# Keys' factor as a logarithm inside the exponent, decays summed per 128 tokens, and bias-fed exponentials for the two coarsest levels, in a gated linear recurrence

## The chip, the cores and the metric

The kernel runs on one core of a Trainium2 chip. The metric is the device time of one execution in microseconds. TensorE (PE) multiplies matrices into PSUM, VectorE (DVE), ScalarE (ACT) and GpSimd (POOL) work on tiles of 128 partitions, and SyncE (SP) issues most of the loads. Every engine takes its own instructions strictly in order.

## The reference

Three transformer blocks run one after the other on 512 tokens of 1024 features. The change touches one branch of the first: a gated linear recurrence with 4 heads of 128 key and 128 value columns, once forward and once backward over the tokens.

```python
def gla_chunkwise(q, k, v, log_f):
    """S_t = diag(f_t) S_{t-1} + k_t v_t^T ; o_t = S_t^T q_t, chunkwise."""
...
        def hgrn_direction(f_logit, lb, reverse):
            f = lb + (1.0 - lb) * jax.nn.sigmoid(f_logit.astype(f32))
            log_f = heads(jnp.log(f), HG_KDIM)
            kh = heads(1.0 - f, HG_KDIM)
            ...
        o_hg = hgrn_direction(f_fw, lb_all[0, layer], False) + hgrn_direction(f_bw, lb_all[1, layer], True)
```

So the weight of token s in the output of token t is a sum over the key columns of q_t times (1 - f_s) times the exponential of a difference of cumulated logarithms of f. All else in the three blocks (latent attention, a mixture of 64 experts, retention, sparse attention, a second recurrence, feed-forwards) is untouched.

## The kernel before

The kernel never walks through the tokens. For each head it builds the whole 512x512 matrix of weights, `At`, by levels. A level L cuts the tokens into pairs of neighbouring blocks of L tokens. Between the two blocks of a pair the decay goes through the pair's middle, so it splits into a factor of the query token and a factor of the key token; the two halves then carry one matmul. Levels 256 and 128 fill the parts of `At` off the diagonal blocks (lines 531 and 537); levels 1, 2, 4, ... 64 fill the four 128x128 blocks on the diagonal (line 551), and `copy_predicated` with a mask (line 556) picks from each level's product the entries that belong to it. A product without any decay, of the queries `q2` and the sum of both directions' keys `ksum` (line 546), gives the diagonal itself.

`hgrn_prepare` does one head's preparation: three column products of the input projection (line 150), the queries `q2`, `sg[d]` = 1 - f for the two directions d (tiles `hs`), the logarithm of f (tiles `hf`, ACT `Ln`, line 482), and its cumulated sum `gs[d]` over all 512 tokens (tiles `hg`, a DVE scan with a zero in front, line 486).

`hgrn_level` makes the factors of one level. Four POOL subtractions of 128x256 (lines 509 and 510) put "middle minus own" or "own minus middle" into `heq` and `hek`, two ACT exponentials of 128x512 follow (lines 511 and 512), and three DVE products: `hq` = queries times `heq` (128x512, line 513) and, for each direction, its half of `hk` = keys times `hek` (128x256, line 515). The four tiles have three buffers each. That is done nine times for each of four heads.

`hgrn_head` runs the levels of a head and their matmuls, moves the sums from PSUM to `At` (ACT, lines 532, 539, 553, 559), and multiplies `At` by the values (line 563). `o_emit` normalizes the head's output with a chain of small DVE instructions and a POOL product (line 634), and PE transposes it (line 639) a little later.

The order around it: `weave` alternates the steps of `hgrn_head` with steps of other PE work, `FILL` (1.4, 1.4, 1.5, 0.5) steps for each step of heads 0 to 3. The other work is the next head's `hgrn_prepare` and then a piece of other products: `mem` products of the second block in heads 0 and 1 (lines 1363 to 1365 and 187 to 189), the `ple` projection in head 2 (lines 187 to 189, evicted by ACT at line 2751), a gate in head 3. Every weight is loaded as `raw` and split into a rounded part `wh` (ACT, line 68) and a rest `wl` (DVE, line 69). A scheduler then sets the final order of each engine's queue from the order in which the code issues; the queues themselves run in order.

Behind the recurrence come the latent attention with the other gates, the merge, the router, and the experts, whose weights `w` are loaded by SP (lines 987 and 996).

## Time and profile before

| | |
|---|---|
| time, median of 3 runs (range) | 3288.96 us (3280.67 to 3289.59) |
| time of the profiled execution | 3286.79 us |
| its span, first to last instruction | 3284.7 us |
| PE, DVE, ACT, POOL busy | 93%, 55%, 31%, 10% of the span |
| the recurrence's four heads | 106.9 to 300.8 us of the span |

PE is busy nearly everywhere, so a microsecond counts only where PE stands still or runs at a lower granted clock. The four heads are one of the few stretches where it does; there POOL, of 10% over the whole span, is nearly always busy. A head is read here from the start of its first level's matmuls, or of the product with the values that closes the head before it, to its own product with the values.

### The profile page before, as it was taken

The page shows a single profiled execution, that of the slowest core. Times are in us where ns is not written, and L with a number is a line of the kernel's source. Part 1 is how long each engine was busy: PE and PEld are TensorE (multiplying, and loading weights), DVE is VectorE, ACT ScalarE, POOL GpSimd, SP SyncE. Part 2 cuts the span into 40 slices and gives each one's busy share as a digit, 9 for nine tenths or more (in the row PEclk, how much of TensorE's full clock was granted, in tenths as well). Part 3 has the DMA queues.
Part 4 walks back from the last instruction along what each step waited for, and adds up shares of the span by engine and source line. Part 5 has one row for each costly group of instructions (what it writes and reads, how often), then busy time and mean ns, then how long its engine had stood idle before and what let it go on. Part 6 is the DMA issues. An engine that isn't in the chain of part 4 may idle for free.

```text
span 3284.7 us, 40559 instructions
## 1 busy us (share of the span) xinstructions
PE 3061.4 (93%) x16321; PEld 2332.6 (71%) x16321; DVE 1790.4 (55%) x3211; ACT 1019.1 (31%) x1550; POOL 337.1 (10%) x395
## 2 busy tenths in 40 slices
PE   9888999788777899999999999999999889999999
PEld 7687777434333688888767778888876767688887
DVE  3777765733432634345974656543477775464443
ACT  3556543110000422223413432322223244232221
POOL 0654101000000000001100320000023210000000
PEclk9889999899888999999999999999999989799999
DMA  4222224699899432333322244323333410123222
GB/s 144 82 71 83 65 65 194 274 421 421 367 421 417 145 102 91 102 105 114 103 90 84 90 154 160 103 91 102 103 95 105 136 51 17 50 90 103 95 91 84
DMA packets 240985, 466.38 MB, mean 142 GB/s; under 512 B 24722, under 2 KB 163380, under 8 KB 216732
## 3 DMA queue, kind: packets, MB, share of 16 engines
q1 hardware_dynamic: 230956, 431.95, 36.5%
q0 software_dynamic: 9840, 31.82, 2.8%
q8 instruction: 130, 2.13, 0.3%
q14 instruction: 59, 0.48, 0.0%
HBM read 441.17 MB, written 22.56 MB: 141 GB/s over the span
## 4 chain that ended last, share of the span: by engine, by line
PE 43%; DVE 6%; issue 1%; ACT 1%; POOL 0%; DMA 0%; DVEq 0%; ACTq 0%; POOLq 0%
PE pg L150 20%; PE pg L188 4%; PE pg L189 4%; PE pg L187 4%; PE pg L2094 1%; DVE wl L69 1%; DVE nprod L2353 1%; PE pt L2084 1%; PE pg L176 1%; PE pg L175 1%; PE pg L174 1%; PE pa L2070 1%; PE pg L2488 1%; PE pg L2487 1%; PE pt L1419 0%
## 5 line engine op out<-in xcount | busy, mean ns | idle before, releaser
L69 DVE TENSOR_TENSOR wl<-raw,wh 128x2048 fp32r<-128x2048 f32 (+3 forms) x211 | 440.2, 2087 | 458.3 <-ACT wh L68 458.2
L68 ACT ACTIVATE wh<-raw 128x2048 fp32r<-128x2048 f32 (+3 forms) x214 | 368.8, 1724 | 703.1 <-PE pg L150 352.0
L150 PE MATMUL pg<-x2h,wh 128*128 128x512 f32 (+2 forms) x1136 | 441.8, 389 | 0.0
L150 PE MATMUL pg<-x2h,wl 128*128 128x512 f32 (+2 forms) x1136 | 440.2, 388 | 0.0
L150 PE MATMUL pg<-x2l,wh 128*128 128x512 f32 (+2 forms) x1136 | 439.2, 387 | 0.0
L150 PEld LDWEIGHTS pg<-x2h,wl 128*128 128x128 f32 (+1 forms) x1136 | 212.8, 187 | 49.2 <-issue 7.3
L150 PEld LDWEIGHTS pg<-x2l,wh 128*128 128x128 f32 (+1 forms) x1136 | 212.8, 187 | 47.6 <-issue 6.4
L150 PEld LDWEIGHTS pg<-x2h,wh 128*128 128x128 f32 (+1 forms) x1136 | 212.9, 187 | 45.6 <-issue 3.0
L188 PE MATMUL pg<-wl,hh 128*128 128x512 f32 x608 | 238.5, 392 | 0.0
L189 PE MATMUL pg<-wh,hl 128*128 128x512 f32 x608 | 237.6, 391 | 0.0
L187 PE MATMUL pg<-wh,hh 128*128 128x512 f32 x608 | 236.6, 390 | 0.0
L1155 PE MATMUL pa<-w,mscr 128*32 128x512 f32 x1024 | 171.0, 669 | 50.4 <-DMA w<-w 48.1
L1155 PEld LDWEIGHTS pa<-w,mscr 128*32 128x32 f32 x1024 | 42.4, 121 | 154.9 <-issue 140.1
L188 PEld LDWEIGHTS pg<-wl,hh 128*128 128x128 f32 x608 | 114.2, 188 | 25.4 <-DVE wl L69 0.8
L187 PEld LDWEIGHTS pg<-wh,hh 128*128 128x128 f32 x608 | 114.1, 188 | 25.1
L189 PEld LDWEIGHTS pg<-wh,hl 128*128 128x128 f32 x608 | 114.2, 188 | 23.8
L187 PE MATMUL pg<-wh,x2h 128*128 128x512 f32 (+1 forms) x288 | 101.5, 353 | 1.0 <-ACT x2h L232 1.0
L189 PE MATMUL pg<-wh,x2l 128*128 128x512 f32 (+1 forms) x288 | 100.8, 350 | 0.0
L188 PE MATMUL pg<-wl,x2h 128*128 128x512 f32 (+1 forms) x288 | 100.4, 349 | 0.0
L150 PE MATMUL pg<-x1h,wh 128*128 128x512 f32 x224 | 90.9, 406 | 1.1 <-ACT po L2751 0.7
L150 PE MATMUL pg<-x1l,wh 128*128 128x512 f32 x224 | 90.9, 406 | 0.0
L150 PE MATMUL pg<-x1h,wl 128*128 128x512 f32 x224 | 90.2, 405 | 0.0
(882 smaller groups left out, 6006.4 us busy)
## 6 DMA issues: line engine op xcount, KB each, us to landing
w<-w SPq DMA_DIRECT2D x188, 1024.0 KB
raw<-w_in SPq DMA_DIRECT2D x45, 1024.0 KB
raw<-ffn_w_in SPq DMA_DIRECT2D x44, 1024.0 KB
raw<-w_ff SPq DMA_DIRECT2D x16, 1024.0 KB
raw<-w_ff SPq DMA_DIRECT2D x20, 768.0 KB
raw<-w_in SPq DMA_DIRECT2D x24, 512.0 KB
raw<-w_out SPq DMA_DIRECT2D x12, 1024.0 KB
raw<-ffn_w_out SPq DMA_DIRECT2D x16, 768.0 KB
```

Of the source, the lines that this page charges most:

```text
L68: nc.scalar.activation(h, t, AF.Copy)
L69: (nc.gpsimd if i in self.slow else nc.vector).tensor_tensor(l, t, f32v(h), op=OP.subtract)
L150: nc.tensor.matmul(p, w[:, c, s], x[:, c, t], start=first, stop=last)
L174: nc.tensor.matmul(p[:, t], wh[:, c, s], xh[:, c, t], start=c == 0, stop=False)
L175: nc.tensor.matmul(p[:, t], wh[:, c, s], xl[:, c, t], start=False, stop=False)
L176: nc.tensor.matmul(p[:, t], wl[:, c, s], xh[:, c, t], start=False, stop=c == nk - 1)
L187: nc.tensor.matmul(p, xh[:, c, t], wh[:, c, :ncol], start=start and c == 0, stop=False)
L188: nc.tensor.matmul(p, xh[:, c, t], wl[:, c, :ncol], start=False, stop=False)
L189: nc.tensor.matmul(p, xl[:, c, t], wh[:, c, :ncol], start=False, stop=stop and c == nk - 1)
L1155: nc.tensor.matmul(ph[s], xt[:, c, s], w[:, :, c], start=c == 0, stop=c == DC - 1)
L2070: mm(ps[s], qT[:, c + 4 * s, i * P:(i + 1) * P], kT[:, s, j, :W], start=j == 0, stop=j == 1)
L2084: nc.tensor.transpose(pt[:, j], prs[s][:, j * P:(j + 1) * P], k.ident)
```

## The change

In `hgrn_prepare` the logarithm of the keys' factor is taken too: `sg[d]` becomes ln(1 - f + 1e-30) (two more ACT `Ln` of 128x512 a head). The cumulated sums restart every 128 tokens: `g` has the shape 128 x 4 x 129, filled by four DVE scans of 128 columns for each direction in place of one of 512, and a tile `htw` of two columns holds the sums of blocks 0 and 1. POOL adds or subtracts these sums and the keys' logarithms once a head (two operations of 128x512), so that `ys` holds the keys' whole exponent but for the middle. `ksum` moves from `hgrn_head` into `hgrn_prepare`.

In `hgrn_level` the keys' factor then comes straight out of the exponential, and the two products of line 515 go. For levels 1 to 64 POOL keeps two subtractions (keys), DVE takes the other two (queries), and two ACT exponentials of 128x512 and one DVE product follow as before. For levels 128 and 256 nothing is subtracted: the middle is the bias of the exponential, in eight ACT instructions of 128x128 for each of the two levels. Results are written in place, so two tile names with four buffers each replace four with three.

```diff
     for d in range(2):
         S.activation(fs[d], fs[d], AF.Ln)
     for d in range(2):
-        g = t(f"hg{d}", (P, T + 1))
-        nc.gpsimd.memset(g[:, 0:1], 0.0)
-        V.tensor_tensor_scan(g[:, 1:], k.one.to_broadcast([P, T]), fs[d], 0.0, op0=OP.mult, op1=OP.add)
+        S.activation(sg[d], sg[d], AF.Ln, bias=k.tiny)
+    two = t("htw", (P, 2))
+    for d in range(2):
+        g = t(f"hg{d}", (P, NT, P + 1))
+        G.memset(g[:, :, 0:1], 0.0)
+        for b in range(NT):
+            V.tensor_tensor_scan(g[:, b, 1:], k.one.to_broadcast([P, P]), fs[d][:, b * P:(b + 1) * P], 0.0,
+                                 op0=OP.mult, op1=OP.add)
+        V.tensor_tensor(two[:, d:d + 1], g[:, 0, P:], g[:, 1, P:], op=OP.add)
         gs.append(g)
-    out.append((q2, sg, gs))
+    G.tensor_tensor(blk(sg[0]), gs[0][:, :, 1:], blk(sg[0]), op=OP.subtract)
+    G.tensor_tensor(blk(sg[1]), gs[1][:, :, 0:P], blk(sg[1]), op=OP.add)
+    out.append((q2, ksum, gs, sg, two))
...
-    for d in range(2):
...
-        G.tensor_tensor(cut(first)[:, :, 0], mid, own[:, :, 0], op=OP.subtract)
-        G.tensor_tensor(cut(second)[:, :, 1], own[:, :, 1], mid, op=OP.subtract)
-    S.activation(eq, eq, AF.Exp)
-    S.activation(ek, ek, AF.Exp)
-    V.tensor_tensor(q, q2, eq, op=OP.mult)
-    for d in range(2):
-        V.tensor_tensor(cut(kk)[:, :, d], cut(ks[d])[:, :, d], cut(ek)[:, :, d], op=OP.mult)
+    if L >= P:
+        for b0 in range(0, NT, 2 * L // P):
+            n = L // P
+            m = b0 + n
+            for b in range(b0, m):
+                e0, e1 = (g[:, b, P:] if b == m - 1 else two[:, d:d + 1] for d, g in enumerate((g0, g1)))
+                S.activation(kb[:, b], y0[:, b], AF.Exp, scale=-1.0, bias=e0)
+                S.activation(qb[:, b], own1[:, b], AF.Exp, scale=-1.0, bias=e1)
+            S.activation(qb[:, m], own0[:, m], AF.Exp)
+            S.activation(kb[:, m], y1[:, m], AF.Exp)
+            if n == 2:
+                S.activation(qb[:, m + 1], own0[:, m + 1], AF.Exp, bias=g0[:, m, P:])
+                S.activation(kb[:, m + 1], y1[:, m + 1], AF.Exp, bias=g1[:, m, P:])
+    else:
...
+        G.tensor_tensor(cut(kb)[:, :, :, 0], mid0, cut(y0)[:, :, :, 0], op=OP.subtract)
+        G.tensor_tensor(cut(kb)[:, :, :, 1], cut(y1)[:, :, :, 1], mid1, op=OP.subtract)
+        V.tensor_tensor(cut(qb)[:, :, :, 0], mid1, cut(own1)[:, :, :, 0], op=OP.subtract)
+        V.tensor_tensor(cut(qb)[:, :, :, 1], cut(own0)[:, :, :, 1], mid0, op=OP.subtract)
+        S.activation(q, q, AF.Exp)
+        S.activation(kk, kk, AF.Exp)
+    V.tensor_tensor(q, q2, q, op=OP.mult)
```

The scheduler makes new queues of this in the four heads; behind them every queue stands as before. Three places follow.

The first place is POOL and DVE at the start of head 0 (levels 256, 128, 1, 2, ... in this order). `hg`, `hs`, `heq` and `hek` are the tiles named above, `hac` is the tile in which the diagonal blocks are collected. POOL before:

```order
L546 TENSOR_TENSOR hks_828<-hs_40_648,hs_41_649 128x512
L509 TENSOR_TENSOR hek_759<-hg_48_752 128x256
L510 TENSOR_TENSOR heq_758<-hg_48_752 128x256
L509 TENSOR_TENSOR hek_798<-hg_48_752 128x2x128
L510 TENSOR_TENSOR heq_797<-hg_48_752 128x2x128
L509 TENSOR_TENSOR heq_758<-hg_49_755 128x256
L510 TENSOR_TENSOR hek_759<-hg_49_755 128x256
```

POOL in the changed kernel:

```order
L484 TENSOR_TENSOR hks_752<-hs_40_650,hs_41_651 128x512
L498 TENSOR_TENSOR hs_40_650<-hg_50_759,hs_40_650 128x512
L499 TENSOR_TENSOR hs_41_651<-hg_51_766,hs_41_651 128x512
L532 TENSOR_TENSOR hek_876<-hg_50_759,hs_40_650 128x256
L533 TENSOR_TENSOR hek_876<-hs_41_651,hg_51_766 128x256
```

Levels 256 and 128 are gone from POOL's queue; two operations of 128x512 stand ahead of level 1, which is the first that POOL serves. DVE before, at the same place:

```order
L486 SCALAR_TENSOR_TENSOR hg_48_752<-one,hf_46_744 128x512
L486 SCALAR_TENSOR_TENSOR hg_49_755<-one,hf_47_747 128x512
L513 TENSOR_TENSOR hq_760<-hq_39_647,heq_758 128x512
L515 TENSOR_TENSOR hk_761<-hs_40_648,hek_759 128x256
L515 TENSOR_TENSOR hk_761<-hs_41_649,hek_759 128x256
```

DVE in the changed kernel:

```order
L494 SCALAR_TENSOR_TENSOR hg_50_759<-one,hf_46_746 128x128 x4
L496 TENSOR_TENSOR htw_758<-hg_50_759 128x1
L494 SCALAR_TENSOR_TENSOR hg_51_766<-one,hf_47_749 128x128 x4
L496 TENSOR_TENSOR htw_758<-hg_51_766 128x1
L538 TENSOR_TENSOR heq_775<-hq_39_649,heq_775 128x512
L534 TENSOR_TENSOR heq_875<-hg_51_766 128x256
L535 TENSOR_TENSOR heq_875<-hg_50_759 128x256
L534 TENSOR_TENSOR heq_900<-hg_51_766 128x128x2
```

Between the scans and level 256's matmuls DVE now has one product where it had three; the subtractions of levels 1 and 2 stand behind it.

The second place is ACT at the end of head 0, where it moves the collected blocks `hac` to `At` (line 559 before, line 580 now), behind exponentials that already belong to head 1. `mo` is an eviction of a `mem` product. Before:

```order
L2737 ACTIVATE mo_1106<-pg_1081 128x256
L512 ACTIVATE hek_1286<-hek_1286 128x512
L511 ACTIVATE heq_1358<-heq_1358 128x512
L512 ACTIVATE hek_1359<-hek_1359 128x512
L511 ACTIVATE heq_1387<-heq_1387 128x512
L512 ACTIVATE hek_1388<-hek_1388 128x512
L2737 ACTIVATE mo_1159<-pg_1134 128x256
L559 ACTIVATE At<-hac_827 128x4x128
```

In the changed kernel, the last wide exponential of head 0 first:

```order
L537 ACTIVATE hek_1165<-hek_1165 128x512
...
L528 ACTIVATE hek_1245<-hs_58_796,hg_85_999 128x128
L522 ACTIVATE hek_1282<-hs_57_795,hg_84_992 128x128
L2760 ACTIVATE mo_1161<-pg_1136 128x256
L523 ACTIVATE heq_1281<-hg_85_999 128x128
L524 ACTIVATE heq_1281<-hg_84_992 128x128
L525 ACTIVATE hek_1282<-hs_58_796 128x128
L522 ACTIVATE hek_1282<-hs_57_795,hg_84_992 128x128
L68 ACTIVATE wh_1266<-raw_1057 128x1024
L580 ACTIVATE At<-hac_840 128x4x128
```

What stands ahead of the eviction were exponentials that read what POOL had just subtracted; now it is 13 narrow ones, whose inputs are made once for the head, two evictions of `mo` and one weight split.

The third place is PE at the same moment: the product with the values reads `At` (line 563 before, line 584 now). Before:

```order
L1364 MATMUL pg_1181<-mhl,wh_1047 128x256
L1365 MATMUL pg_1181<-mhl,wl_1048 128x256
L531 MATMUL pa_1259<-hq_1248,hk_1249 128x256
L563 MATMUL pg_1210<-hv,At 128x128 x16
L531 MATMUL pa_1259<-hq_1248,hk_1249 128x256
L531 MATMUL pa_1263<-hq_1248,hk_1249 128x256 x2
```

In the changed kernel:

```order
L572 MATMUL pa_1124<-heq_1115,hek_1116 128x128 x4
L572 MATMUL pa_1173<-heq_1164,hek_1165 128x128 x4
L1387 MATMUL pg_1179<-mhl,wh_1053 128x256
L1388 MATMUL pg_1179<-mhl,wl_1054 128x256
L1386 MATMUL pg_1179<-mhl,wh_1053 128x256
L1387 MATMUL pg_1179<-mhl,wh_1053 128x256
L1388 MATMUL pg_1179<-mhl,wl_1054 128x256
L554 MATMUL pa_1255<-heq_1244,hek_1245 128x256 x2
L554 MATMUL pa_1259<-heq_1244,hek_1245 128x256 x2
L584 MATMUL pg_1208<-hv,At 128x128 x16
```

All four of head 1's first matmuls now stand ahead of head 0's product with the values, where one stood; the last two levels of head 0 stand later among the `mem` products than they did.

## Rows read from the trace of the kernel before

**Rows 1.** The page's first line: the span.

```profile
span 3284.7 us, 40559 instructions
```

**Rows 2.** Busy time by stretch, heads 0 to 3: length, busy (count), clock, DMA.

```profile
core 0: us, PE busy (x) PEld busy (x) DVE busy (x) ACT busy (x) POOL busy (x), PEclk, DMA share, GB/s
106.92:160.64 53.72, 37.53 (x224) 33.60 (x224) 47.57 (x56) 30.33 (x49) 45.25 (x57) 0.85 0.18 53
160.64:217.32 56.68, 48.46 (x283) 44.12 (x283) 40.83 (x61) 29.88 (x44) 32.17 (x39) 0.86 0.23 70
217.32:280.06 62.74, 54.30 (x292) 47.38 (x293) 49.93 (x77) 40.15 (x67) 47.31 (x56) 0.93 0.24 71
280.06:300.84 20.78, 19.06 (x118) 16.54 (x117) 14.95 (x38) 9.37 (x28) 5.89 (x5) 1.00 0.40 136
```

**Rows 3.** PE in order of time: start, us, what, [idle before, releaser].

```profile
111.89 3.78 PE L531 MATMUL pa<-hq,hk 128*128 128x256 f32 x8 [4.97 <-DVE hk L515]
...
160.64 6.00 PE L563 MATMUL pg<-hv,At 128*128 128x128 f32 x32 [6.58 <-ACT At L559]
...
176.28 1.11 PE L639 MATMUL pt<-ident,osq 128*128 128x128 f32 x4 [3.09 <-POOL osq L634]
...
269.78 0.50 PE L187 MATMUL pg<-wh,phl 128*128 128x512 f32 x1 [3.10 <-ACT po L2751]
...
280.06 3.74 PE L563 MATMUL pg<-hv,At 128*128 128x128 f32 x32
```

**Rows 4.** DVE, POOL, ACT by line: ns shortest/median/longest, first and last start, form.

```profile
L513 DVE TENSOR_TENSOR hq<-hq,heq x36: 655/844/1121, 110.1 to 295.3; 128x512 f32<-128x512 f32 x36
L515 DVE TENSOR_TENSOR hk<-hs,hek x72: 395/828/1526, 111.0 to 296.9; 128x256 f32<-128x256 f32 x72
L486 DVE TENSOR_TENSOR_SCAN hg<-one,hf x8: 1203/1216/2295, 103.3 to 256.4; 128x512 f32<-128x512 f32 x8
L509 POOL TENSOR_TENSOR hek<-hg x36: 607/792/2661, 105.6 to 284.6; 128x256 f32<-128x256 f32 x36
L546 POOL TENSOR_TENSOR hks<-hs,hs x4: 1282/1680/3320, 103.6 to 254.5; 128x512 f32<-128x512 f32 x4
L511 ACT ACTIVATE heq<-heq x36: 612/630/638, 109.4 to 283.3; 128x512 f32<-128x512 f32 x36
L539 ACT ACTIVATE At<-pa x16: 258/278/301, 118.6 to 274.5; 128x128 f32<-128x128 f32 x16
L482 ACT ACTIVATE hf<-hf x8: 630/632/637, 102.6 to 255.7; 128x512 f32<-128x512 f32 x8
L482 ACT ACT_TABLE_LOAD  x6: 1283/1283/1283, 101.3 to 254.4; - x6
L511 ACT ACT_TABLE_LOAD  x4: 1283/1283/1283, 104.1 to 257.1; - x4
```

**Rows 5.** Start of head 0, DVE and ACT in order of time.

```profile
103.33 3.38 DVE L486 TENSOR_TENSOR_SCAN hg<-one,hf 128x512 f32<-128x512 f32 x2
...
109.42 0.63 ACT L511 ACTIVATE heq<-heq 128x512 f32<-128x512 f32 x1 [4.04 <-POOL heq L509]
...
110.08 0.99 DVE L513 TENSOR_TENSOR hq<-hq,heq 128x512 f32<-128x512 f32 x1 [3.38 <-ACT heq L511]
```

**Rows 6.** End of head 0, DVE and ACT in order of time.

```profile
156.52 0.72 DVE L556 COPY_PREDICATED hac<-lev,pa 128x512 f32<-128x512 int32 x1
...
157.66 0.63 ACT L511 ACTIVATE heq<-heq 128x512 f32<-128x512 f32 x1 [2.55 <-POOL heq L509]
...
159.97 0.62 ACT L559 ACTIVATE At<-hac 128x512 f32<-128x512 f32 x1
```

**Rows 7.** Behind the heads: a wait in SP's queue, and two stretches (columns of rows 2).

```profile
SPq L987 <- PE pg L189: 26.0, 1, 26.0
...
580.00:600.00 20.00, 10.67 (x71) 10.31 (x71) 19.27 (x41) 0.80 (x2) 0.00 (x0) 0.62 0.22 93
900.00:1000.00 100.00, 82.24 (x512) 40.07 (x512) 35.71 (x56) 8.87 (x15) 0.00 (x0) 0.90 1.01 421
```

35 lines of the change are left out of this document (18 added, 17 removed).

## The prediction

> **What bounds the kernel now.** I read first the busy time by stretch, because PE is busy 93% of the span and only a stretch where it stands can give anything back. Over heads 0 to 3 the length less PE's busy time is 16.2, 8.2, 8.4 and 1.7 us, together 34.6 [rows 2]. The granted clock is 0.85, 0.86 and 0.93 there, so part of the busy time ran at 1.2 instead of 2.4 GHz: busy time times the missing share is 37.5 x 0.15 = 5.6, 48.5 x 0.14 = 6.8 and 54.3 x 0.07 = 3.8 us, together 16.2 [rows 2]. Read it off one product: the 32 matmuls with the values take 6.00 us behind a wait of 6.58 us, and 3.74 us where PE came out of steady work [rows 3]. So 34.6 + 16.2 = 50.8 us is all that any change of these heads could give.
>
> Next, who lets PE wait. The order in time names DVE's keys product at the start (4.97 us), ACT's copy into `At` at the end of head 0 (6.58), POOL's product before the transposes (3.09), ACT's eviction `po` (3.10) [rows 3]. Behind these names stands one pair: in head 0 DVE is busy 47.6 and POOL 45.3 of 53.7 us, in head 2 49.9 and 47.3 of 62.7 [rows 2]. The ACT waits lead back to it too: the last masked copy of head 0 ends at 157.24, yet its move to `At` starts at 159.97, because an exponential ahead of it in ACT's queue had waited 2.55 us for POOL [rows 6]. And the two lengthen each other: a 128x256 product on DVE takes 0.395 us at best and 0.828 as a rule, a 128x512 one 0.655 and 0.844, a POOL subtraction 0.607 and 0.792 [rows 4].
>
> **POOL's part.** A head now has 36 subtractions and one sum: 36 x 0.792 + 1.68 = 30.2 us. It keeps 14 subtractions and gets three operations of 128x512 priced as the sum: 14 x 0.792 + 3 x 1.68 = 16.1 [rows 4]. 14 us a head go; they are no term of the sum by themselves, since PE never waits for POOL alone, but they halve what DVE collides with.
>
> **DVE's part.** At unchanged durations a head has 9 x 0.844 + 18 x 0.828 + 2 x 1.216 = 24.9 us of products and scans [rows 4]. Of the 18 half products none stay, and 14 half subtractions come, of the same form and count of inputs, so at the same 0.828. A scan of 128 columns is not in the trace: a quarter of 1.203 is 0.30, and a quarter of the longest, 2.295, is 0.57. Between 256 and 512 columns the products grow by 0.26 us, which leaves 0.135 fixed; that gives (1.203 - 0.135) / 4 + 0.135 = 0.40, near the lower end, and 0.135 for each of two one-column sums. So 9 x 0.844 + 14 x 0.828 + 8 x 0.40 + 0.3 = 22.7: 2.2 us less a head; with 0.57 it is 0.9 less, with 0.30 it is 3.0.
> Then the collisions. The excess over the shortest is 9 x 0.189 + 14 x 0.433 = 7.8 us in the new list. With POOL at 16.1 / 30.2 = 53% of its work I take 53% of it, 4.1: another 3.6 us less. It is nothing if the two still meet as often, and 7.8 if they never meet. DVE's head gets shorter by 5.8 us (0.9 to 10.8).
>
> **Head 0** runs at DVE's pace, so the 5.8 us count whole. Its start: the second scan ended at 106.7, then POOL's subtractions let ACT start at 109.42, and PE started at 111.89 [rows 3, 5]. Now eight scans end at about 107.5 (103.33 + 8 x 0.40 + 0.3, and some collision with the sum on POOL). POOL's sum runs from 103.6 until 105.3; of its two new operations the second has to await the scans and ends at 109.2, at 1.68 [rows 4]. Four logarithms from 102.6 on and the table load, 4 x 0.632 + 1.283 [rows 4], end at 106.4 and hold nothing up. The eight narrow exponentials, 0.278 each, of which the last three wait for the second operation, end at 110.0, the queries' product at 110.7. That is 1.2 us earlier than 111.89; with POOL at its shortest 1.28 us it is 2.5. I take 1.5. Four column matmuls stand ahead of it now, which fill part of the wait and are missing later: nothing. Its end: of the 2.7 us between masked copy and move to `At` I take 1.5, since 13 narrow exponentials (13 x 0.278 = 3.6 us, fed once a head) stand where eight POOL-fed ones stood. And half of the clock's 5.6, 2.8, for waits that get short. Together 5.8 + 1.5 + 1.5 + 2.8 = 11.6.
>
> **Heads 1 and 2** don't run at DVE's pace throughout (40.8 of 56.7 and 49.9 of 62.7 us busy [rows 2]); the normalization's chain of small instructions, ACT's evictions and PE's own work take their share. I take half of PE's standing, 4.1 and 4.2, and a third of the clock, 2.3 and 1.3: 6.4 and 5.5. **Head 3** has 1.7 us in all: nothing.
>
> **ACT's part.** Added are 8 logarithms of 0.632 us, 64 narrow exponentials of 0.278 in place of 16 wide ones of 0.63, and two table loads of 1.283, since the new logarithms stand apart from the exponentials of levels 16 to 64 in two heads: 5.1 + 7.7 + 2.6 = 15.4 us in 194 us in which ACT is busy 110 [rows 2, 4]. Most lies beside PE's filling products. On the path are the loads at the end of heads 0 and 2, where the last levels' exponentials follow them: 2.6 if both end last, 0 if the `mem` and `ple` products cover them. I take 1.5.
> The trace shows a load of 1.283 us ahead of logarithms six times and ahead of exponentials four times [rows 4], so each change between the two costs one here. The Trainium skill (ScalarE: Activation LUTs, section "Table sets: the hidden batching unit") says that one set holds exponential and logarithm together and that the pair needs one load. By that rule the two new loads would be free and the term would be 0; the rows speak otherwise, and the sum goes by them.
>
> **What it meets later.** Nothing behind the heads is reordered. The first load of expert weights waits 26.0 us for a matmul of PE, the DMA is at 0.22 of its share while PE stands for the router, and only then the experts run at 421 GB/s [rows 7]. So a load-bound stage follows, but it starts when PE gets there, and what the heads gain stays gained.
>
> **Sum.** 11.6 + 6.4 + 5.5 - 1.5 = 22.0 us. The profiled execution took 3286.79 us, 2.1 more than its span of 3284.7 [rows 1] and 2.2 less than the median of 3288.96: 3286.8 - 22.0 = 3264.8, so **3265 us**. Taking DVE's ends (0.9 and 10.8 for 5.8 in head 0, and a quarter or three quarters of the standing of heads 1 and 2), the same working gives 3252 to 3276.
>
> **Rivals.** *The pair takes turns (faster still).* The best durations next to the usual ones say that DVE and POOL hardly run side by side at all. If so, their shortest durations add up: before, POOL 36 x 0.607 + 1.28 = 23.1 and DVE 9 x 0.655 + 18 x 0.395 + 2 x 1.203 = 15.4, 38.5 us a head; after, 14 x 0.607 + 3 x 1.28 = 12.3 and 9 x 0.655 + 14 x 0.395 + 8 x 0.40 + 0.3 = 14.9, 27.2 [rows 4]. Three heads shorter by 11.3 each, the start's 1.5 and half of the clock's 16.2 are 43.5: 3243 us. Against it: in head 1 PE is busy 48.5 of 56.7 us and cannot lose 11 without the clock [rows 2]. Chance 0.12.
> The Trainium skill (SBUF — State Buffer, section "Who interferes with whom") states this as a rule: a DVE instruction with two SBUF inputs and a GpSimd instruction that reads SBUF exclude each other for the whole instruction. The rows' 0.395 against 0.828 us agree with waiting, but no row shows that it is for the whole of it. By the same rule DVE's new subtractions stay in the collision, which speaks against a change that only moves work from POOL to DVE.
>
> *It moves the work only (no change).* POOL's 14 us go, but DVE still has 25 instructions a head that meet POOL, and keeps its place as the queue that ends last. Then only the 0.9 us a head of three heads with dear scans and the start's 1.2 remain, less 1.5 on ACT: 2.4 us, 3284. For it: DVE stands for only 6.1 of head 0's 53.7 us, 3.4 of them at the start [rows 2, 5]. Chance 0.20.
>
> *ACT ends last (slower).* At each of three head ends the move to `At` stands behind 13 narrow exponentials, two `mo` and a weight split. If POOL's two new operations for the next head come late (they queue behind the old head's level 64), the whole group runs after them: 3.6 + 0.8 + 1.0 = 5.4 us, and 1.3 for a table load, 6.7 at three ends, 20.1 us; against it the start, 1.5, and DVE's gain in head 0 of 5.8, with clock 2.0: 10.8 slower, 3298. It decides from where the product with the values waits more than some 4 us for ACT at all three ends; in head 0 it does so already. Against it: ACT has 84 idle us in the heads [rows 2]. Chance 0.08.
>
> **How the numbers follow.** The forecast has 0.60. About 0.3%, 10 us, is what a measurement of this kernel can tell from no change. Faster by more: the forecast and the taking of turns, 0.72; within: 0.20; slower: 0.08. The range has to reach into the no-change case and half into the fast one: 3245 to 3285 leaves out 0.08 slow, half of 0.12 fast and a quarter of 0.20.
>
> **What will show it.** Right: PE's standing over the heads falls from 34.6 to about 17 us; POOL is busy half as long; the half subtractions on DVE have a median near 0.6 us; a 128-column scan takes about 0.4; `At` at the end of head 0 makes PE wait under 3 us. Wrong: subtractions on DVE at 0.83 and PE's waits unchanged (no change), waits of PE for ACT's move to `At` of over 4 us at three ends (slower), or a first expert load that doesn't come earlier by what the heads gained.

## The result, and the profile after

The changed kernel takes 3264.51 us (median of 5 runs, 3260.15 to 3269.12), the kernel before 3282.08 us beside it (5 runs): a ratio of 0.994 with a 95% interval of 0.9923 to 0.9958. The forecast was 3265 us, with a range of 3245 to 3285, so the time and the sign came as predicted. That the time came within half a microsecond is luck: the forecast took 22.0 us from a profiled execution of 3286.79 us, while the kernel before has a median of 3282.08 us beside the change, and by medians the change saves 17.6 us. The profiled execution took 3260.15 us, 1.75 more than its span and the fastest of the five.

First the same four stretches as in [rows 2], each from one product with the values to the next; columns as there.

```profile
core 0: us, PE busy (x) PEld busy (x) DVE busy (x) ACT busy (x) POOL busy (x), PEclk, DMA share, GB/s
106.92:149.98 43.06, 36.70 (x230) 32.78 (x228) 39.47 (x60) 36.15 (x72) 21.46 (x25) 0.92 0.24 71
149.98:202.18 52.20, 44.43 (x286) 40.01 (x285) 38.73 (x67) 33.58 (x63) 23.75 (x20) 0.97 0.24 72
202.18:258.06 55.88, 49.81 (x285) 42.50 (x285) 44.78 (x83) 40.87 (x80) 27.53 (x28) 0.97 0.27 86
258.06:278.25 20.19, 19.07 (x118) 16.55 (x117) 13.39 (x34) 11.40 (x32) 4.08 (x3) 1.00 0.35 122
```

The stretches got shorter by 10.7, 4.5, 6.9 and 0.6 us, 22.6 in all. PE's standing, length less busy time, went from 16.2, 8.2, 8.4 and 1.7 to 6.4, 7.8, 6.1 and 1.1: 13.3 less. PE's busy time went from 37.5, 48.5, 54.3 and 19.1 to 36.7, 44.4, 49.8 and 19.1 for nearly the same matmuls (917 and 919 records in all, up to 7 more or fewer in a stretch): 9.3 less, at granted clocks of 0.92, 0.97 and 0.97 in place of 0.85, 0.86 and 0.93. POOL's busy time is 76.8 instead of 130.6 us, ACT's 122.0 instead of 109.7.

PE in order of time, with the idle time before an instruction in brackets:

```profile
110.79 3.44 PE L554 MATMUL pa<-heq,hek 128*128 128x256 f32 x8 [3.05 <-DVE heq L538]
...
149.98 3.83 PE L584 MATMUL pg<-hv,At 128*128 128x128 f32 x32
...
162.25 0.66 PE L662 MATMUL pt<-ident,osq 128*128 128x128 f32 x4 [2.50 <-POOL osq L657]
...
192.29 0.98 PE L572 MATMUL pa<-heq,hek 128*128 128x128 f32 x3 [3.85 <-DVE heq L538]
```

Against [rows 3]: the start waits 3.05 us where it waited 4.97, and head 0's product with the values (L584, formerly L563) no longer waits 6.58 us for ACT's move into `At`. The longest wait now stands in the middle of head 1 (3.85 us at 192.29), and it is a new one.

DVE, POOL and ACT by line (shortest/median/longest in ns), to be held against [rows 4]:

```profile
L538 DVE TENSOR_TENSOR heq<-hq,heq x36: 675/681/1354, 110.0 to 265.8; 128x512 f32<-128x512 f32 x36
L534 DVE TENSOR_TENSOR heq<-hg x28: 401/418/1411, 110.6 to 263.5; 128x256 f32<-128x256 f32 x28
L535 DVE TENSOR_TENSOR heq<-hg x28: 409/414/1095, 111.6 to 264.6; 128x256 f32<-128x256 f32 x28
L494 DVE TENSOR_TENSOR_SCAN hg<-one,hf x32: 391/398/1503, 103.2 to 239.4; 128x128 f32<-128x128 f32 x32
L532 POOL TENSOR_TENSOR hek<-hg,hs x28: 624/830/2750, 109.3 to 258.4; 128x256 f32<-128x256 f32 x28
L522 ACT ACTIVATE hek<-hs,hg x12: 386/388/396, 108.6 to 243.6; 128x128 f32<-128x128 f32 x12
L525 ACT ACTIVATE hek<-hs x12: 292/298/313, 109.4 to 246.4; 128x128 f32<-128x128 f32 x12
```

The medians jump from near the usual duration to the shortest one, which flatters: the longest are as long as before. The means tell more. They stand in the view that groups by line (busy us, mean ns of one):

```profile
L538 DVE TENSOR_TENSOR heq<-hq,heq 128x512 f32<-128x512 f32 x36 | 26.5, 757 | 8.1 <-ACT heq L536 3.8 <-ACT heq L527 2.0 <-ACT heq L523 1.6
L534 DVE TENSOR_TENSOR heq<-hg 128x256 f32<-128x256 f32 x28 | 18.1, 647 | 0.4 <-PE pa L572 0.4
L535 DVE TENSOR_TENSOR heq<-hg 128x256 f32<-128x256 f32 x28 | 16.6, 593 | 0.0
L494 DVE TENSOR_TENSOR_SCAN hg<-one,hf 128x128 f32<-128x128 f32 x32 | 16.4, 573 | 2.4 <-ACT hf L486 2.4
```

The same view of the kernel before:

```profile
L513 DVE TENSOR_TENSOR hq<-hq,heq 128x512 f32<-128x512 f32 x36 | 31.4, 873 | 9.9 <-ACT heq L511 7.1 <-PE pa L537 2.8
L515 DVE TENSOR_TENSOR hk<-hs,hek 128x256 f32<-128x256 f32 x72 | 50.3, 726 | 0.0
L486 DVE TENSOR_TENSOR_SCAN hg<-one,hf 128x512 f32<-128x512 f32 x8 | 11.7, 1478 | 0.0
```

Behind the heads the gain stays: the first load of expert weights, at 524.0 us before, is issued at 501.2, 22.8 earlier (SP's issues by line, before and then after; first and last start behind the durations):

```profile
L987 SPq DMA_DIRECT2D w<-w x128: 327/376/810, 524.0 to 1041.5; - x128
```

```profile
L1010 SPq DMA_DIRECT2D w<-w x128: 327/376/818, 501.2 to 1020.7; - x128
```

From the product with the values of head 3 to that first load the traces of all 14 kernels take 223.0 to 224.8 us; from there to the end the same code, in the same order on PE, DVE and ACT, takes 2754 to 2769 us, over 14 us of difference that no edit made. So the experiments are judged by the heads first: **the gain** of a kernel is how much earlier than in the kernel before its products with the values of heads 0, 1, 2 and 3 start, both counted from the first matmul. The changed kernel has 10.7, 15.1, 22.0 and 22.6 us. Each gain is read from one traced execution; how much it varies between executions of one kernel was not measured.

The scheduler gives most of these kernels another order as well, and the gain of an edit then includes that of the order. Counted from 100 us to the product with the values of head 3, 42 of ACT's 249 instructions stand elsewhere with three buffers than in the change, and 42 of 191 in the kernel before with its subtractions on DVE. The two kernels with idle work have the order of the kernel with all four subtractions on DVE (one place of ACT's apart), and moving the normalization's product to DVE changes few places (5 of PE's 942). So these comparisons are the clean ones.

### The profile page after: what moved, and what is told of

Same layout as the page of the kernel before. It is cut to its first block, busy times and chain, and to the rows that moved or that the text cites. A ratio compares the mean times of both kernels' runs of the same rounds, so it can differ in the third digit from the quotient of the medians.

```text
span 3258.4 us, 40500 instructions
## 1 busy us (share of the span) xinstructions
PE 3044.4 (93%) x16321; PEld 2319.7 (71%) x16321; DVE 1773.7 (54%) x3227; ACT 1033.1 (32%) x1608; POOL 282.8 (9%) x316
## 4 chain that ended last, share of the span: by engine, by line
PE 43%; DVE 6%; issue 1%; ACT 1%; POOL 0%; DMA 0%; DVEq 0%; ACTq 0%; POOLq 0%
PE pg L150 20%; PE pg L188 4%; PE pg L189 4%; PE pg L187 4%; DVE nprod L2376 1%; DVE wl L69 1%; PE pg L2117 1%; PE pt L2107 1%; PE pg L176 1%; PE pg L175 1%; PE pg L174 1%; PE pa L2093 1%; PE pt L1442 0%; PE pg L2511 0%; PE pg L2510 0%
```

## The experiments

| kernel | gain at heads 0, 1, 2, 3 (us) | median (us) | ratio to before, 95% interval |
|---|---|---|---|
| the change | 10.7, 15.1, 22.0, 22.6 | 3264.51 | 0.994 (0.9923 to 0.9958) |
| biases only | 8.0, 13.7, 12.7, 12.8 | 3267.68 | 0.9958 (0.9941 to 0.9974) |
| log only | 3.9, 6.6, 6.6, 5.8 | 3284.24 | 1.0007 (0.9995 to 1.0019) |
| all four subtractions on DVE | 7.2, 17.0, 25.8, 25.8 | 3254.18 | 0.9919 (0.9902 to 0.9936) |
| all four subtractions on POOL | 6.5, 11.1, 13.1, 7.2 | 3279.76 | 0.9985 (0.9974 to 0.9996) |
| all on DVE, idle subtractions on POOL | -5.1, -2.1, -6.1, -13.9 | 3301.66 | 1.0043 (1.0028 to 1.0058) |
| all on DVE, idle fills on POOL | 8.7, 17.7, 26.5, 25.2 | 3259.07 | 0.992 (0.9891 to 0.995) |
| nothing on POOL in the recurrent part | 11.4, 23.1, 31.4, 31.3 | 3255.00 | 0.9904 (0.988 to 0.9928) |
| and the norm's product on DVE | 12.5, 25.1, 35.3, 36.0 | 3250.73 | 0.9897 (0.9876 to 0.9917) |
| three buffers a factor | 10.7, 11.5, 19.7, 17.7 | 3265.59 | 0.9947 (0.9931 to 0.9962) |
| no logarithm | 5.6, 9.4, 16.2, 12.8 | 3267.86 | 0.9945 (0.9928 to 0.9963) |
| before, subtractions on DVE | 8.9, 19.4, 28.0, 19.2 | 3269.71 | 0.9944 (0.9926 to 0.9962) |
| log in tiles of its own | 9.7, 14.7, 20.0, 20.1 | 3266.92 | 0.9952 (0.9935 to 0.9968) |

### One part of the change alone

**Biases only.** The kernel before, with the middles of levels 256 and 128 as biases and the keys' products left on DVE:

```
+    neg = t("hng", (P, 2, 3))
+    for d in range(2):
+        V.tensor_scalar(neg[:, d], gs[d][:, P:T:P], -1.0, None, op0=OP.mult)
...
+        if L >= P:
+            for c in range(T // (2 * L)):
+                at = (2 * c + 1) * L
+                S.activation(cut(first)[:, c, 0], own[:, c, 0], AF.Exp, scale=-1.0, bias=g[:, at:at + 1])
+                S.activation(cut(second)[:, c, 1], own[:, c, 1], AF.Exp, bias=neg[:, d, at // P - 1:at // P])
+            continue
```

> The kernel before with only the two coarsest levels changed: middles as biases of the exponential (own minus middle with a negated copy of three columns a direction), cumulated sums over all 512 tokens and the keys' product as before. POOL loses 8 of 36 subtractions a head, nothing comes to DVE but two tiny products. Theory A (DVE's excess from collisions with POOL, and the clock, carry the gain): POOL's share falls to 78%, DVE's excess of 7.9 us a head by 1.7, the start of head 0 comes 2 us earlier: heads end 6 to 8 us earlier, time 6 us less than before. Rival B (the gain is the coarse levels' chain at each head's start and end, where ACT waited behind POOL): 15 us or more of the 22.6.

Measured: a gain of 12.8 us at head 3, between the two. The first level starts 3.3 us earlier than before, more than in the whole change (1.1). Here the exponentials follow the scan and the negated columns directly.

**Log only.** The kernel before, with the log of the keys' factor inside the exponent on all nine levels, two subtractions on POOL and two on DVE, and the scans of 512 columns kept:

```
-    V.tensor_tensor(q, q2, eq, op=OP.mult)
-    for d in range(2):
-        V.tensor_tensor(cut(kk)[:, :, d], cut(ks[d])[:, :, d], cut(ek)[:, :, d], op=OP.mult)
+    G.tensor_tensor(cut(kk)[:, :, 0], mid0, cut(ys[0])[:, :, 0], op=OP.subtract)
+    G.tensor_tensor(cut(kk)[:, :, 1], cut(ys[1])[:, :, 1], mid1, op=OP.subtract)
+    V.tensor_tensor(cut(q)[:, :, 0], mid1, cut(own1)[:, :, 0], op=OP.subtract)
+    V.tensor_tensor(cut(q)[:, :, 1], cut(own0)[:, :, 1], mid0, op=OP.subtract)
...
+    V.tensor_tensor(q, q2, q, op=OP.mult)
```

> The kernel before with only the keys' logarithm in the exponent: per level two subtractions on POOL, two on DVE, two wide exponentials, one product, for all nine levels; sums over 512 tokens in one scan, no biases. POOL has 18 subtractions and three wide operations a head, about 60% of before; DVE's count stays at 27. Theory A: DVE's excess of 7.9 us a head falls by some 3, and the clock gives as much again in heads 0 to 2: heads end 10 to 13 us earlier. Rival B (coarse chain): under 6 us, since levels 256 and 128 still pass POOL and now await the logarithms too.

Measured: 5.8 us at head 3, and no difference in the time. That is rival B's side (under 6) and half of what theory A gave. ACT's waits between 100 and 310 us show what holds it (engine, what waited for what: us in all, times, longest):

```profile
ACT hek L512 <- POOL hek L508: 43.7, 21, 5.5
```

POOL makes the keys' differences, and ACT stands for them 21 times, nearly as long as for all four differences in the kernel before (46.2 us from the start of the heads to head 3's product with the values). That points at POOL as a link in the chain to the exponentials, beside the collisions. Taken apart, biases and log give 12.8 + 5.8 = 18.6 of the 22.6 us. The biases carry the larger part: they take 8 of 36 subtractions a head from POOL at the two levels that open a head.

### Where the subtractions stand

**All on DVE, all on POOL.** The changed kernel, with one engine for all four subtractions of a level from 64 down:

```
-        G.tensor_tensor(cut(kb)[:, :, :, 0], mid0, cut(y0)[:, :, :, 0], op=OP.subtract)
-        G.tensor_tensor(cut(kb)[:, :, :, 1], cut(y1)[:, :, :, 1], mid1, op=OP.subtract)
+        V.tensor_tensor(cut(kb)[:, :, :, 0], mid0, cut(y0)[:, :, :, 0], op=OP.subtract)
+        V.tensor_tensor(cut(kb)[:, :, :, 1], cut(y1)[:, :, :, 1], mid1, op=OP.subtract)
```

and the other way round for the second kernel.

> The changed kernel with all four subtractions of levels 1 to 64 on DVE, POOL left with three wide operations a head. Theory A: DVE's list grows by 14 x 0.405 = 5.7 us a head and its excess of about 5 falls to 1 or 2: DVE's head grows by 2, heads end within 4 us of the changed kernel's. Rival C (collisions count little, the number of DVE instructions sets the pace): DVE's head grows by 14 x 0.62 = 8.7 us, heads end 12 to 20 us later than the changed kernel's, about as before. In both the half subtractions' mean falls to 0.42 us only if POOL is what lengthens them.

> The changed kernel with all four subtractions of levels 1 to 64 on POOL. DVE loses 14 instructions a head, POOL has 28 subtractions and three wide operations, nearly as before. Theory A: DVE's list is 5.7 us shorter, but the rest collides more and each exponential again awaits four POOL subtractions in a row: heads end 8 to 14 us later than the changed kernel's. Rival C (DVE's list sets the pace): heads end 10 us earlier than the changed kernel's, 32 earlier than before.

Measured: 25.8 us with all on DVE, 7.2 with all on POOL, 15.4 later than the change where 8 to 14 were expected. DVE executes 14 instructions a head more in the first than in the change and is earlier all the same; it executes 14 fewer in the second and is later. So the number of DVE's instructions alone doesn't set the pace. With all on POOL, ACT waits for POOL on either factor and the queries' product takes 909 ns on the mean; with all on DVE it takes 686, and the half subtractions 416 to 452 (the columns are those of the second view by line above).

```profile
L538 DVE TENSOR_TENSOR heq<-hq,heq 128x512 f32<-128x512 f32 x36 | 24.4, 686 | 9.4 <-ACT heq L536 4.8 <-ACT heq L527 3.7 <-ACT heq L524 0.5
L534 DVE TENSOR_TENSOR heq<-hg 128x256 f32<-128x256 f32 x28 | 12.7, 452 | 0.0
L535 DVE TENSOR_TENSOR heq<-hg 128x256 f32<-128x256 f32 x28 | 11.7, 417 | 0.0
```

What stayed open: whether POOL harms only as a slow link in each level's chain, or also by being busy beside DVE.

**Idle work on POOL.** Two kernels test that. Both are the one with all four subtractions on DVE, with instructions on POOL in addition whose results nobody reads; what PE, DVE and ACT execute, and in which order, is untouched. In the first, POOL subtracts:

```
+        x = pool.tile([P, NT, P // 2], FT, name=k.nm("hx"), tag="hx", bufs=2)
+        for _ in range(2):
+            G.tensor_tensor(x, g0[:, :, 0:P // 2], g1[:, :, 1:P // 2 + 1], op=OP.subtract)
+            G.tensor_tensor(x, g1[:, :, 0:P // 2], g0[:, :, 1:P // 2 + 1], op=OP.subtract)
```

> This is the variant with all four subtractions on DVE, plus four idle subtractions of 128x256 per fine level on POOL (28 a head, reading both cumulated decays, writing a tile that nobody reads); the order on PE, DVE and ACT is untouched, and POOL's idle work is in nobody's chain. Collision theory: POOL costs time by being busy beside DVE. In the changed kernel 14 subtractions on POOL a head went with DVE's half subtractions at 0.59 to 0.65 us instead of 0.42 to 0.45, about 3.7 us a head; 28 should bring them to 0.65 or more, some 7 us a head on DVE, and the gain at the product with the values of head 3 falls from 25.8 to under 18 us. Chain theory: POOL costs time only as a slow link of each level. Then the durations may rise, but the gain stays above 23 us.

In the second it fills:

```
+        x = pool.tile([P, T], FT, name=k.nm("hx"), tag="hx", bufs=2)
+        G.tensor_tensor(x[:, 0:1], g0[:, 0, 0:1], g1[:, 0, 1:2], op=OP.subtract)
+        for _ in range(4):
+            G.memset(x, 0.0)
```

> The same variant with four fills of 128x512 per fine level on POOL in place of the idle subtractions (28 a head, which read nothing), behind one subtraction of one column each that holds them to their level. If it is reading operands beside DVE that lengthens DVE's instructions, the fills cost nothing: half subtractions on DVE at 0.42 to 0.46 us and a gain within 2 us of 25.8 at the product with the values of head 3. If any busy POOL lengthens them, the durations rise as with the idle subtractions, to 0.55 us or more, and the gain falls under 20 us.

Measured: with the subtractions the gain of 25.8 us turns into a loss of 13.9, the kernel is slower than the one before (1.0043); with the fills it stays at 25.2. The first kernel by line, DVE and POOL:

```profile
L542 DVE TENSOR_TENSOR heq<-hq,heq 128x512 f32<-128x512 f32 x36 | 32.3, 904 | 4.7 <-ACT heq L527 3.4 <-ACT heq L540 1.2
L581 DVE COPY_PREDICATED hac<-lev,pa 128x512 f32<-128x512 int32 x28 | 20.6, 737 | 20.9 <-PE pa L576 20.8
L534 DVE TENSOR_TENSOR heq<-hg 128x256 f32<-128x256 f32 x28 | 18.9, 676 | 0.0
L535 DVE TENSOR_TENSOR heq<-hg 128x256 f32<-128x256 f32 x28 | 18.4, 656 | 0.0
...
L538 POOL TENSOR_TENSOR hx<-hg,hg 128x256 f32<-128x256 f32 x56 | 49.8, 905 | 1.7 <-DVE htw L496 1.4
```

and the second:

```profile
L542 DVE TENSOR_TENSOR heq<-hq,heq 128x512 f32<-128x512 f32 x36 | 24.6, 689 | 11.1 <-ACT heq L527 4.7 <-ACT heq L540 3.3 <-ACT heq L524 2.9
L534 DVE TENSOR_TENSOR heq<-hg 128x256 f32<-128x256 f32 x28 | 12.0, 430 | 0.0
L535 DVE TENSOR_TENSOR heq<-hg 128x256 f32<-128x256 f32 x28 | 11.9, 424 | 0.0
...
L539 POOL MEMSET hx<- 128x512 f32 x112 | 54.9, 527 | 0.7
```

The four half subtractions have means of 429 ns without the idle work, 663 with subtractions beside them and 437 with fills. So 112 x 0.234 + 36 x (0.904 - 0.686) = 34.0 us of DVE time come from nothing but POOL's reading beside it, of the 39.7 us that the gain loses. One idle POOL subtraction costs the path 39.7 / 112 = 0.35 us; the same subtraction on DVE takes 0.42. DVE's whole account says the same. From the start of the heads to head 3's product with the values (columns of [rows 2]), first without the idle work and then with the idle subtractions:

```profile
106.92:275.08 168.16, 150.64 (x914) 132.38 (x913) 134.27 (x296) 121.86 (x243) 21.29 (x19) 0.95 0.28 84
```

```profile
106.92:314.77 207.85, 164.44 (x913) 142.63 (x912) 174.60 (x296) 122.68 (x243) 118.58 (x131) 0.88 0.22 68
```

The same 296 instructions of DVE take 40.3 us more, and DVE stands as long as before (33.9 and 33.3 us). The fills keep POOL busy for 112 x 0.527 = 59 us, the subtractions for 112 x 0.904 = 101; the 8 ns by which fills lengthen the half subtractions, against 234, are far less than that ratio would give. The collision theory holds, and the chain theory falls as the only cause, at its own bound of 23 us. That POOL costs nothing as a link is not shown by these kernels, since none of their levels goes through POOL.

How it looks in order of time, DVE first and then POOL, in head 0 of the first kernel (start us, length us):

```profile
119.60 0.86 DVE L533 TENSOR_TENSOR hek<-hs,hg 128x256 f32<-128x256 f32 x1
120.39 0.86 DVE L534 TENSOR_TENSOR heq<-hg 128x256 f32<-128x256 f32 x1
121.17 0.86 DVE L535 TENSOR_TENSOR heq<-hg 128x256 f32<-128x256 f32 x1
...
127.80 0.86 DVE L471 TENSOR_SCALAR hs<-hs 128x512 f32<-128x512 f32 x1
128.58 0.72 DVE L581 COPY_PREDICATED hac<-lev,pa 128x512 f32<-128x512 int32 x1
```

```profile
119.36 0.82 POOL L539 TENSOR_TENSOR hx<-hg,hg 128x256 f32<-128x256 f32 x1
120.15 1.61 POOL L538 TENSOR_TENSOR hx<-hg,hg 128x256 f32<-128x256 f32 x2
121.72 1.42 POOL L539 TENSOR_TENSOR hx<-hg,hg 128x256 f32<-128x256 f32 x2
```

DVE's instructions start 0.79 and 0.78 us apart (119.60, 120.39, 121.17) and POOL's 0.79 (119.36, 120.15, then two in 1.57): one each in the same 0.785 us, in step. From start to start, half subtractions in a row take DVE 0.335 us in the kernel without idle work, and POOL's idle ones 0.600 at their fastest. That is 0.935 together, so the two take turns for all but 0.15 us of a pair.
The Trainium skill (SBUF — State Buffer, section "Who interferes with whom") says that a DVE instruction with two SBUF inputs contends with a GpSimd instruction that reads SBUF and not with one that only writes it. The runs agree: 663 and 437 ns. It calls this an exclusive lock; whether the 0.15 us are a gap in the lock or the part of each instruction that reads nothing, no run here separates.

**Nothing on POOL.** The keys' sum and the two operations on the log keys on DVE as well, then the normalization's product too:

```
-    G.tensor_tensor(ksum, sg[0], sg[1], op=OP.add)
+    V.tensor_tensor(ksum, sg[0], sg[1], op=OP.add)
...
-    G.tensor_tensor(blk(sg[0]), gs[0][:, :, 1:], blk(sg[0]), op=OP.subtract)
-    G.tensor_tensor(blk(sg[1]), gs[1][:, :, 0:P], blk(sg[1]), op=OP.add)
+    V.tensor_tensor(blk(sg[0]), gs[0][:, :, 1:], blk(sg[0]), op=OP.subtract)
+    V.tensor_tensor(blk(sg[1]), gs[1][:, :, 0:P], blk(sg[1]), op=OP.add)
...
-                G.tensor_tensor(sq, sq, og[:, :, h * P:(h + 1) * P], op=OP.mult)
+                V.tensor_tensor(sq, sq, og[:, :, h * P:(h + 1) * P], op=OP.mult)
```

(the last pair in the second kernel alone)

> The variant with all four subtractions on DVE, with the keys' sum and the two operations on the log keys on DVE as well, so that POOL has only the normalization's products beside DVE in these heads. Collision theory: DVE gets three instructions of 0.66 us a head (2.0 us), and loses the excess of the scans and products that ran beside POOL's 128x512 operations of 1.2 to 2.1 us: about even at the heads' ends, 24 to 28 us of gain, and half subtractions at 0.40 to 0.43 us. The start of head 0 gets earlier, since the two operations take 1.3 us in place of 2.4 to 3 us. If DVE's instruction count counted, the gain would fall by 2 us a head, to under 21.

> The variant without POOL in the recurrent part, with the normalization's product of 128x512 on DVE too (0.69 us there, 1.37 us on POOL, behind which PE's transposes wait 0.8 to 2.5 us). The path of the normalization gets 0.7 us shorter a head, DVE's list 0.69 us longer: a gain of 30 to 34 us at the product with the values of head 3, where the variant without it has 31.3, and a time of 3250 to 3256 us. If DVE's instruction count sets the pace by now, the gain falls under 30 us.

Measured: 31.3 and 36.0 us at head 3, both above what was expected, and 3255.00 and 3250.73 us. The second beats both kernels of the case, by 1.0% against the one before. The two differ by the normalization's product alone, in nearly the same order, and that product is worth 4.7 us at head 3. The second kernel's stretches, cut as above to within a microsecond:

```profile
105.00:148.00 43.00, 37.30 (x237) 33.17 (x236) 41.38 (x87) 38.85 (x77) 0.21 (x2) 0.96 0.36 106
148.00:192.00 44.00, 42.33 (x286) 38.45 (x285) 35.61 (x77) 31.20 (x52) 0.21 (x2) 1.00 0.22 62
192.00:244.70 52.70, 48.63 (x278) 41.82 (x276) 44.78 (x108) 40.51 (x83) 0.77 (x1) 0.97 0.27 83
244.70:264.70 20.00, 19.70 (x124) 17.52 (x125) 16.56 (x43) 12.90 (x34) 1.31 (x2) 1.00 0.44 142
```

PE stands for 11.7 us over the four, where it stood for 34.6 in the kernel before. In the second stretch, that of head 1, DVE executes 77 instructions in 35.6 us where it executed 67 in 38.7 in the change, and PE stands 1.7 us where it stood 7.8.

**The kernel before, subtractions on DVE.** Nothing of the change; only the engine of the 36 subtractions a head:

```
-        G.tensor_tensor(cut(first)[:, :, 0], mid, own[:, :, 0], op=OP.subtract)
-        G.tensor_tensor(cut(second)[:, :, 1], own[:, :, 1], mid, op=OP.subtract)
+        V.tensor_tensor(cut(first)[:, :, 0], mid, own[:, :, 0], op=OP.subtract)
+        V.tensor_tensor(cut(second)[:, :, 1], own[:, :, 1], mid, op=OP.subtract)
```

> The kernel before with its 36 subtractions a head on DVE in place of POOL, nothing else. Collision theory: a 128x256 subtraction on POOL costs DVE and the path about 0.35 us (112 idle ones cost 39.7 us), one on DVE costs 0.42 us, so DVE's work grows by 36 x 0.07 = 2.5 us a head while POOL leaves the chain of each level: DVE, 153 us busy in the heads, loses some 33 us of excess and gets 144 x 0.42 = 60 us, 180 of 194 us. About even: a gain of -5 to 12 us at the product with the values of head 3, half products at 0.40 to 0.43 us. If taking POOL out of the chain were the whole of what the variants gain, and the logarithm and the biases nothing, it would be 18 us or more.

Measured: 19.2 us at head 3 (28.0 at head 2), and 3269.71 us, a ratio of 0.9944 where the change has 0.994. I had expected about even; by the bound set ahead, 18 us or more, this is the result of the other reading, that taking POOL out of the chain is what gains. DVE's own rows are as expected (means of 449 ns for the half products and 413 to 440 for the subtractions). From the start of the heads to head 3's product with the values, in the kernel before and then in this one:

```profile
106.92:300.84 193.92, 159.36 (x913) 141.64 (x914) 153.27 (x228) 109.73 (x186) 130.62 (x155) 0.89 0.24 73
```

```profile
106.92:281.67 174.75, 148.31 (x914) 130.92 (x913) 165.51 (x380) 108.87 (x187) 16.00 (x11) 0.97 0.27 81
```

DVE's work grew by 12.2 us, near the 10 that a price of 0.07 us for each of 144 subtractions gives; the 180 us of the expectation took too little for the collisions that end. The gain comes from DVE's standing, which fell from 40.7 to 9.2 us: before, ACT's exponentials waited 46.2 us for POOL's subtractions in this stretch, and here none waits. So POOL cost the kernel before time both ways, in collisions and as a link in each level; how much of the standing went by the other order is not shown. In the change the two parts are 16.9 us less of DVE's busy time (153.3 to 136.4) and 5.7 us less of its standing.

So moving the work alone brings at head 3 nearly what the change brings, and as much in the whole time. Head 3 gives back 9 of the 28 us: its stretch takes 29.6 us where it took 20.8, 2.5 of it for 14 more matmuls that stand in it now, 6.3 for standing of PE (8.0 for 1.7 us), behind the normalizations' small instructions and POOL's product in them, ACT's evictions and its move to `At`. What the logarithms and biases add once DVE subtracts is 25.8 - 19.2 = 6.6 us in the heads; with POOL's sums on DVE as well it is 31.3 - 19.2 = 12.1. Both differences include the other order.

### Waits and buffers

**Three buffers.** The changed kernel with `bufs=3` for `heq` and `hek`.

> The changed kernel with three buffers in place of four for the queries' and the keys' factors of a level. POOL waited 34 us in the heads for PE to release the keys' buffer, with no wait of PE behind it. If the lookahead over the levels carries part of the gain, the gain at the product with the values of head 3 falls by 4 us or more below 22.6; if not, it stays within 2 us.

Measured: 17.7 us at head 3, 4.9 less; head 1 loses 3.6 and head 3 2.6, head 2 gives 1.3 back. By its own bound the lookahead over the levels is a part of the gain, though no wait of PE for a buffer shows it; the changed order is not told apart from it. In the whole time it can't be told apart from the change (0.9947 against 0.994).

**No logarithm.**

```
-        S.activation(fs[d], fs[d], AF.Ln)
+        S.activation(fs[d], fs[d], AF.Identity, scale=-0.02)
...
-        S.activation(sg[d], sg[d], AF.Ln, bias=k.tiny)
+        S.activation(sg[d], sg[d], AF.Identity, scale=-0.02, bias=k.tiny)
```

> The changed kernel with the four logarithms of a head replaced by scalings of the same tiles (identity times -0.02), so that what follows computes other values; no table load is left between logarithms and exponentials (13 loads of 1.283 us, 16.7 us of ACT), and a few instructions of the levels change places. The forecast put two of the loads on the path, 1.5 us in all. If loads at the heads' ends are on the path, the gain at the product with the values of head 3 rises from 22.6 by 3 us or more; if PE's filling products cover them, as the waits of the changed kernel suggest (none of PE for ACT at a head's end), it stays within 2 us.

Measured: the loads are gone, and the gain is 12.8 us, 9.8 less than with them, which neither of the two readings had; the whole time shows no difference (0.9945 against 0.994). The largest of PE's waits between 100 and 300 us is new against the change:

```profile
PE pg L584 <- ACT At L580: 8.3, 3, 5.1
```

At the end of head 0 (2.6 us of it) the instructions that changed places put an exponential that waits 2.94 us for POOL ahead of the move into `At` again, as in the kernel before [rows 6]. At the end of head 1 (5.1 us) the move waits for DVE's last masked copy, which stands behind a weight split of 2.93 us. In these heads the changed order cost more than the 13 table loads gave back; what the loads cost at an unchanged order stays open.

**Log in tiles of its own.** In the change the logarithm is written over the keys' factors that POOL's sum reads, and so has to wait for it. In head 1 that is where the 3.85 us come from, by POOL's and ACT's rows in order of time:

```profile
184.58 3.26 POOL L484 TENSOR_TENSOR hks<-hs,hs 128x512 f32<-128x512 f32 x1 [5.33 <-DVE hs L481]
```

```profile
187.87 1.34 ACT L488 ACTIVATE hs<-hs,tiny 128x512 f32<-128x512 f32 x2 [1.81 <-POOL hks L484]
...
189.49 1.28 ACT L536 ACT_TABLE_LOAD   x1
190.79 0.63 ACT L536 ACTIVATE heq<-heq 128x512 f32<-128x512 f32 x1
```

The sum takes 3.26 instead of 1.28 us beside a weight split and scans of DVE; the logarithms wait for it, the next level's exponential follows behind a table load, DVE's product and PE behind that. The edit:

```
+    ys = [t(f"hy{d}") for d in range(2)]
...
-        S.activation(sg[d], sg[d], AF.Ln, bias=k.tiny)
+        S.activation(ys[d], sg[d], AF.Ln, bias=k.tiny)
```

with `ys` in the two operations and the levels.

> The changed kernel with the keys' logarithms and the two operations on them in tiles of their own (two buffers a direction), so that they don't wait until POOL's sum has read the keys' factors; some instructions change places. In the changed kernel PE's longest wait after the start, 3.85 us in head 1, goes back through an exponential and a table load to ACT's logarithms, which started 1.81 us late, after a sum of 3.26 us on POOL. If this new wait costs what that chain shows, it is gone: no wait of a logarithm for the sum, the wait of PE in head 1 under 2.5 us, and 1.5 to 4 us more gain at the products with the values of heads 1 to 3 (16.5 to 19 at head 1, 15.1 in the changed kernel). If the table load and the scans set that moment anyway, the gains stay within 1.5 us.

Measured: the wait of the logarithms is gone, PE's longest wait for a level's product (L573 there) is 1.6 us, and the gains are 14.7, 20.0 and 20.1, within 0.5 us of the change at head 1 and 2 to 2.5 below it behind. In its place PE waits 2.2 us each for a weight's two halves, and ACT's wait for POOL's differences has gone from 17.3 to 23.0 us. The wait was real, and yet removing it gave nothing. At the same place ACT's changed order has a weight split of 1.89 us ahead of the table load, so the level's exponential starts at 192.24 us, later than the 190.79 of the change; what the wait costs at an unchanged order is not shown.

## Why the prediction was right, step by step

- **What bounds the heads**: right. Of the 50.8 us of standing and clock that any change could win, 22.6 came. That POOL's reading lengthens DVE's instructions and the path is shown by the idle work; that the pair stood behind most of PE's waits, by the kernel with nothing on POOL, where 11.7 of 34.6 us of standing are left.
- **POOL's part**, no term of the sum: the step "PE never waits for POOL alone" was too strong. Its own rows have PE wait 3.09 us for POOL's normalization product, and that product moved to DVE gave 4.7 us. And POOL as a link, which the prediction left out, shows in the kernel before with its subtractions on DVE, whose gain goes with 31.4 us less standing of DVE.
- **DVE's part**, 5.8 us a head: too large. By means the list went from 9 x 0.873 + 18 x 0.726 + 2 x 1.478 = 23.9 us to 9 x 0.757 + 14 x 0.62 + 8 x 0.573 + 0.5 = 20.6, 3.3 less. In head 0, the only place where the sum uses it, all of DVE's busy time fell by 8.1 us (47.6 to 39.5), so there the too large price of the list did no harm. Two terms were mis-sized. I took medians for "as a rule", and the list of before is 24.9 by them and 23.9 by means; and the new scans, forecast at 0.40, have that as a median (0.398) and 0.573 as a mean, since they meet POOL's sum and operations: 8 x 0.17 = 1.4. At the shortest durations the two lists are nearly equal (15.4 and 9 x 0.675 + 14 x 0.405 + 8 x 0.391 + 0.3 = 15.2): the change saves DVE collisions and hardly any work. The collisions themselves were right: 4.1 us of excess forecast for the products and subtractions that are left, 9 x 0.082 + 14 x 0.215 = 3.7 measured.
- **Head 0**, 11.6: 10.7. Start 1.5 forecast, 1.1 came (its faster case, 2.5, adds up to 1.6). The wait at the end, of which I took 1.5, is gone with all its 6.58 us: it wasn't a term beside DVE's 5.8 but the place where that shows. The clock gave 0.8 in place of 2.8.
- **Heads 1 and 2**, 6.4 and 5.5: 4.5 and 6.9, from other sources. I took half of the standing; in head 1 only 0.4 of 8.2 us went, in head 2 2.4 of 8.4, for new waits stood up, the 3.85 us first. And I took a third of the clock, 2.3 and 1.3; PE's busy time fell by 4.0 and 4.5. So standing was forecast at 15.6 with ACT's part and gave 13.3, the clock at 6.4 and gave 9.3: the two errors cancel, and the sum of 22.0 against 22.6 is better than its terms, which is luck.
- **Head 3**: 0 forecast, 0.6 came.
- **ACT's part**, -1.5: not separated. One table load stands on the chain of the 3.85 us (189.49), none at a head's end. The trace has 13 loads for logarithms and exponentials, three more than before, each where one follows the other; the Trainium skill (ScalarE: Activation LUTs, section "Table sets: the hidden batching unit"), by which the pair needs one load, is not borne out by this trace either. The narrow exponentials were priced at 0.278, 17.8 us for all 64, and keep ACT busy for 17.6: one with a tile as bias lasts 0.388, but in a row they overlap and follow each other by 0.29, those without by 0.20. ACT's busy time rose by 12.3 us (15.4 forecast).
- **What it meets later**: right, the first expert load comes 22.8 us earlier.
- **The signs**: standing at 21.3 us (17 forecast); POOL at 76.8 of 130.6 us, 59% where half was forecast; half subtractions with medians of 0.414 and 0.418 (0.6 forecast) though means of 0.593 and 0.647; `At` at the end of head 0 without a wait.
- **The rivals**: *The pair takes turns* has the mechanism right, and the step 0.785 us of two instructions shows it; the time it gave, 3243, didn't come: heads 1 and 2 got 4.5 and 6.9 us shorter and not 11.3 each, in head 1 for the reason named against it, too little standing. *It moves the work only* rested on moved work gaining nothing, and that is false: moving all 36 subtractions a head with nothing else of the change gave 19.2 us. *ACT ends last* didn't arise in the change. The kernel without logarithms has PE wait 5.1 us for the move into `At` at one end, but there ACT itself waits for DVE.
- **The range**: the ends named for 3252 to 3276 add up to 3256 and 3274 (22.0 + 5.0 + 4.2 and 22.0 - 4.9 - 4.2 us off 3286.8); the chances and the wider range don't rest on them.

## What to carry to other kernels

An instruction on POOL that reads SBUF beside a busy DVE isn't free: price it at least at what it takes from DVE (here 0.35 of the 0.42 us that DVE itself would need), and move work there only where DVE stands idle or where POOL merely writes. Add what waits for it: where ACT and PE follow POOL in each level, as in the kernel before, the moved subtractions gave 19.2 us although DVE's own work grew. Read means beside medians where two engines collide, since a median jumps from one end to the other while the sum moves little. A wait that ends last in a trace is a candidate and not a gain; it counts once the kernel without it is timed.
